# Half of an output projection's first pass placed behind a recurrent scan, and its weights' low parts made on another engine, in a one-core hybrid decoder kernel

## The chip, the cores and the metric

The kernel runs on one core of one Trainium2 chip. The metric is device time in microseconds (us). The engines are named as in the profile: PE (TensorE, matrix products; PEld are its weight loads), DVE (VectorE), ACT (ScalarE), POOL (GpSimd) and SP (SyncE, which here only issues DMAs).

## What is computed

One decoder layer over 512 tokens of width 1024, in float32. A combined input projection feeds three groups of heads side by side; their outputs are concatenated to `y` (512 x 1024) and go through one output projection with a residual, then a squared-ReLU MLP with a residual:

```
h = rms_norm(x, norm_mix[l])
proj = h @ w_in[l]
y_a = gdn_mixer(...)     # 6 heads, gated DeltaNet: a scan over 8 chunks of 64 tokens
y_b = nsa_mixer(...)     # 6 heads of attention: compressed, selected and window branches
y_c = pool_mixer(...)    # 256 columns, causal pooling
y = concatenate([y_a, y_b, y_c], axis=-1)
x = x + y @ w_out[l]
h = rms_norm(x, norm_ffn[l])
x = x + square(relu(h @ w_ffn1[l])) @ w_ffn2[l]
```

Of the columns of `y`, row blocks 0 to 2 of `w_out` (128 rows each) meet the DeltaNet's columns, blocks 3 to 5 the attention's, and blocks 6 and 7 the pooling's.

## The kernel before

A float32 product is made of three products of split operands: each operand is a high part (a cast, on ACT) and a low part (the rest, a subtraction), and the kernel sums high x high, high x low and low x high. So each weight that is loaded goes through a raw buffer, a cast on ACT and a subtraction, before PE can use it.

The program has three stretches. Up to some 233 us PE projects the tokens and solves the DeltaNet's triangular systems (`slabs`, `preps`, `solves`). From there to some 372 us three tracks share the engines: the end of the DeltaNet's scan (`gdn_step`, nine steps, of which steps 4 to 8 fall here), then `gdn_out` for four row tiles of 128 tokens; the attention (`attentions`, `probs`, `values`); and the output projection (`out_gdn`). After that the MLP runs with PE full.

A step of the scan makes six groups of small products on one PSUM bank: `ps` is started (L895, L899), `vn` is copied out by DVE (L903), the next state is made (L912, L915), and the outputs are summed (L920) and copied to `vb` by ACT (L924). `gdn_out` takes a tile of `vb`, normalizes it (L934 to L938, with the tiny steps of `rsqrt` on L103 to L111), multiplies it by the gate on POOL (L939), transposes it on PE into bank 3 (L942), and splits it into `yTh` and `yTl` (L147 on ACT, L148 on DVE), column by column.

The output projection goes in three passes, `PASS = [(6,7),(0,1,2),(3,4,5)]`, each a list of row blocks of `w_out`. A pass has eight tiles (four row tiles by two column halves `hf`); a tile is three products of 128x512 for each block (L1247 in `out_mm`) in one bank, added to `x2` by DVE (L1252). The first pass needs nothing of the scan or the attention; the second needs the DeltaNet's `yTh`, `yTl`.

The weights are loaded by `load_w`: a DMA (L1217) into one of two raw buffers of the pool `wr`, a cast on ACT (L1219), and the low part. For blocks 0 to 5 and for the first two slabs of `w_ffn1` (mode "AG") the low part is two POOL subtractions of 128x512 (L1223); for blocks 6 and 7 (mode "AV") it is one DVE subtraction of 128x1024 (`split`, L134). The parts live in two pools: `wo4` (two blocks) lies beside the DeltaNet's memory `gd`, and `wo6` (three blocks) in memory that `gd` gives back. Before, blocks 4 to 7 are in `wo4`, blocks 0 to 3 in `wo6`.

The order of the instructions on each engine is set by a list scheduler when the program is built: `side_by_side((42, attentions()), (27, out_gdn()))` sets priorities, and the scheduler places each instruction by its own estimate of time. Every engine then runs its list strictly in that order. `tc.issue_after(ins)` orders the instructions that are traced inside it, on the engine of `ins`, behind `ins`; `keep_in_program_order` does the same for a chain.

The lines that the prediction names: L134, L147, L148 (splits), L110 and L111 (`rsqrt`), L895 to L924 (`gdn_step`), L938 to L942 (`gdn_out`), L1097 (compressed probabilities), L1116 to L1122 (scores, their maximum and their exponential), L1145 and L1161 (transposes and value products), L1217 to L1223 (`load_w`), L1247 and L1252 (output products and their additions).

Of the kernel before, what the change touches and what calls it, by code (L numbers as in the profile page):

```python
# [16 lines left out]
ALU = mybir.AluOpType  # L17
# [3 lines left out]
P = 128  # L21
# [16 lines left out]
def trunk_kernel(ctx, tc, x, norm_mix, w_in, conv_w, a_log, dt_bias, gdn_norm, nsa_q_norm, nsa_k_norm,  # L38
# [844 lines left out]
    def gdn_step(t, St):  # L883

        sides = []
        for a in range(2):
            if 0 <= t - a < 2 * NT:
                i, p = divmod(t - a, 2)
                sides.append((grp[i], i, halves[p], halves[1 - p], 3 * a, slice(a, H, 2)))
        rows, nrows = (slice(0, P), slice(0, P)) if len(sides) == 2 else sides[0][2:4]  # L890
        ps = ps_()
        p3 = ps[:, 0:384].rearrange("p (a s c) -> p a s c", a=2, s=3)
        for j in range(3):
            for d, i, h, nh, s0, hs in sides:
                PE.matmul(ps[h, ts(j, HD)], d["TT"][h, s0 + j], vb[h, i, hcol(s0 + j)], start=(j == 0), stop=False,  # L895
                          skip_group_check=True)
        for j in range(3):
            for d, i, h, nh, s0, hs in sides:
                PE.matmul(ps[h, ts(j, HD)], kr[h, i, s0 + j], St[h, j], start=False, stop=(j == 2),  # L899
                          skip_group_check=True)  # L900
        yield 0.4
        vn = w1t([P, 3, HD], "vn")
        V.tensor_copy(vn[rows], p3[rows, 0])  # L903
        Sn = St
        if t < 2 * NT:
            gls = w1t([P, 3, HD], "gls")
            Sn = w1t([P, 3, HD], "S")
            for d, i, h, nh, s0, hs in sides:
                G.tensor_tensor(gls[nh], St[h], egc[h, 2, i, hs].unsqueeze(2).to_broadcast([64, 3, HD]), ALU.mult)
            for j in range(3):  # L910
                for d, i, h, nh, s0, hs in sides:
                    PE.matmul(ps[nh, 192 + HD * j:192 + HD * j + HD], qr[h, i, hcol(s0 + j)], vn[h, j], start=True, stop=True)  # L912
            if t == 0:
                V.memset(Sn[sides[0][2]], 0.0)
            V.tensor_tensor(Sn[nrows], p3[nrows, 1], gls[nrows], ALU.add)  # L915
            yield 0.2
        for a_ in range(2):
            for j in range(3):
                for d, i, h, nh, s0, hs in sides:
                    PE.matmul(ps[h, ts(j, HD)], (d["qdT"][h, s0 // 3, j], d["QK"][h, s0 + j])[a_],  # L920
                              (St[h, j], vn[h, j])[a_], start=(j == 0 and a_ == 0), stop=(j == 2 and a_ == 1),
                              skip_group_check=True)
        for d, i, h, nh, s0, hs in sides:
            S.copy(vb[h, i, hs], p3[h, 0])  # L924
        yield 0.4
        return Sn
# [70 lines left out]
        yield from proj_tok([(0, win[:, 2572:2700]), (128, win[:, 1152:1280])], vw)  # L997
        yield from proj_tok([(0, win[:, 1280:1536])], lambda ps: gate_z(128, ps, ps))

    grp, have = {}, set()  # L1000

    def until(*names):
        while not have.issuperset(names):
# [56 lines left out]
    wr = ctx.enter_context(pool("wr", 2, side="right"))  # L1060
    nwe = ExitStack()
    nw = nwe.enter_context(pool("nw", 2, side="right"))
    wop = [nwe.enter_context(pool("wo4", 4, side="right"))]
    gd.close()
    wop.append(nwe.enter_context(pool("wo6", 6, side="right")))
    fe = ExitStack()
    wq = fe.enter_context(pool("wq", 2))

# [141 lines left out]
    def load_w(pl_, view, tag, e):  # L1210
# [3 lines left out]
        for k in range(0, n, 1024 // m):  # L1214
            k = slice(k, k + 1024 // m)
            r = wr.tile([P, 1024 // m, m], F32, tag="raw", name=nm("raw"))
            SY.dma_start(r, view[:, k])  # L1217
            if e == "AG":
                S.copy(hi[:, k], r)  # L1219
                for d in [(k, slice(d, d + 512)) for d in range(0, m, 512)] if m > 512 else \  # L1220
                        [(slice(q, q + 512 // m), slice(0, m)) for q in range(k.start, k.stop, 512 // m)]:
                    rd = r[:, d[0].start - k.start:d[0].stop - k.start, d[1]]
                    G.tensor_tensor(lo[:, d[0], d[1]], rd, f32v(hi[:, d[0], d[1]]), ALU.subtract)  # L1223
            else:
                split([(r, k)], hi, lo, e)
        return hi, lo

    def load_wo(*cs):
        for c in cs:
            wo[c] = load_w(wop[c < 4], w_out[0, ts(c, P), :].unsqueeze(1), "wo", "AG" if c < 6 else "AV")  # L1230

    w1s = []
    PASS = [(6,7),(0,1,2),(3,4,5)]

    def load_w1(q):
        return load_w(wq, w_ffn1[0, :, 256 * q:256 * q + 256].rearrange("(k p) n -> p k n", p=P), "w1",
                      "AG" if q < 2 else "AV")

    po = banks(4, 5), banks(4, 5, 6), banks(4, 5, 0, 1)

# [23 lines left out]
        begun.append(po[2]())  # L1264
        out_mm(begun[g_], PASS[-1], 0, 2, g_ // 2, g_ % 2, kp)

    def out_part(cl, hf):

        for i in range(NT):
            out_tile(cl, i, hf)  # L1270
            yield 0.64 * len(cl)

    def out_gdn():
        for cl in PASS[:-1]:
            load_wo(*cl)
            if cl is PASS[0]:
                for i in range(NT):
                    SY.dma_start(x2[i], x[0, ts(i, P), :])
            yield from until(*(("y", c) for c in cl if 2 < c < 6))
            for hf in range(2):  # L1280
                yield from out_part(cl, hf)
        load_wo(*PASS[-1])
        have.add("w_out")
        w1s.extend(load_w1(q) for q in range(2))

# [197 lines left out]
```

## Time and profile before

| what | value |
|---|---|
| median of 3 runs | 715.31 us (715.3 to 715.41) |
| the profiled execution | 715.41 us |
| its span, first to last instruction | 713.7 us |
| granted TensorE clock, mean | 0.994 of full speed |
| PE busy | 692.7 us, 97% of the span |
| DVE, ACT, POOL busy | 76%, 55%, 28% of the span |

The profiled execution is 1.7 us longer than its span, and 0.1 us above the median. A row of the timeline gives start, duration, engine, line, operation, output<-inputs, shape and count, and in brackets the idle time before it and what ended it. A row of the windows gives, for a stretch, its length, then busy time and number of instructions of PE, PEld, DVE, ACT and POOL, then the granted clock, the DMA engines' busy share, and GB/s.

### The profile page before, as it was taken

The numbers are of one execution on the slowest core, as the hardware profiler recorded it, in microseconds if no ns is written. First come the engines' busy times: TensorE is split into PE (matmuls) and PEld (weight loads), VectorE is DVE, ScalarE is ACT, GpSimd is POOL, SyncE is SP. The second block draws the span as 40 slices with busy tenths as digits, with TensorE's granted clock in tenths as the row PEclk, the third lists the DMA queues.
The fourth block names the chain that finished last, engine by engine and source line by source line (L and its number), as shares of the span: only waits on it lengthen the run. The fifth ranks groups of instructions, "written<-read, shape, count | busy, mean of one in ns | idle before, by whom it ended". The sixth has DMA issues, their size and how long they took to land.

```text
span 713.7 us, 13238 instructions
## 1 busy us (share of the span) xinstructions
PE 692.7 (97%) x5137; PEld 567.4 (80%) x5137; DVE 544.8 (76%) x999; ACT 392.4 (55%) x786; POOL 200.9 (28%) x277
## 2 busy tenths in 40 slices
PE   8999999999999997999999999999999999999997
PEld 8888777999888775676679888888888888888885
DVE  6688998877786879566566996968878586886836
ACT  5465845665773577388575664446355534635440
POOL 6820023223134013343030242505041230504123
PEclk9999999999999999899999999999999999999999
DMA  7343223133213301211210614233140523322103
GB/s 225 97 133 89 70 51 90 32 108 107 76 32 130 110 1 32 88 59 60 89 54 37 196 71 135 71 119 118 60 141 36 163 73 119 118 60 76 43 1 118
DMA packets 49921, 62.19 MB, mean 87 GB/s; under 512 B 5494, under 2 KB 42564, under 8 KB 49860
## 3 DMA queue, kind: packets, MB, share of 16 engines
q1 hardware_dynamic: 48996, 61.16, 27.4%
q8 instruction: 40, 0.66, 0.4%
q10 hardware_dynamic: 864, 0.20, 0.1%
q14 instruction: 21, 0.17, 0.1%
HBM read 59.25 MB, written 2.10 MB: 86 GB/s over the span
## 4 chain that ended last, share of the span: by engine, by line
PE 85%; DVE 7%; ACT 4%; issue 2%; DMA 2%; POOL 1%; SPq 0%; DVEq 0%; ACTq 0%
PE ps L1344 25%; PE ps L143 10%; PE ps L142 10%; PE ps L144 10%; PE ps L434 6%; PE ps L1247 5%; PE ps L815 3%; PE ps L1161 3%; PE ps L1145 2%; PE ps L260 2%; PE ps L1116 1%; PE ps L603 1%; DMA raw<-in_w_in_dram 1%; PE ps L1117 1%; PE ps L920 1%
## 5 line engine op out<-in xcount | busy, mean ns | idle before, releaser
L1344 PE MATMUL ps<-h2l,hw 128*128 128x512 f32 (+1 forms) x280 | 104.8, 374 | 0.4 <-DVE h2l L1323 0.4
L1344 PE MATMUL ps<-h2h,hw 128*128 128x512 f32 (+1 forms) x280 | 105.2, 376 | 0.0
L1344 PE MATMUL ps<-h2h,lw 128*128 128x512 f32 (+1 forms) x280 | 104.9, 375 | 0.0
L1371 POOL TENSOR_TENSOR al<-gF,ah 128x512 fp32r<-128x512 f32 x24 | 34.3, 1429 | 226.7 <-ACT ah L1370 183.6
L142 PE MATMUL ps<-bh,ah 128*128 128x512 f32 x224 | 88.2, 394 | 0.5 <-DVE x L1452 0.5
L143 PE MATMUL ps<-bl,ah 128*128 128x512 f32 x224 | 88.1, 393 | 0.0
L1452 DVE TENSOR_TENSOR x<-ps,x 128x512 f32<-128x512 f32 x112 | 73.2, 682 | 18.7 <-PE ps L144 18.6
L144 PE MATMUL ps<-bh,al 128*128 128x512 f32 x224 | 84.9, 393 | 0.0
L1364 DVE TENSOR_TENSOR bl<-w2r,bh 128x1024 fp32r<-128x1024 f32 x40 | 57.4, 1436 | 5.6 <-ACT bh L1363 5.6
L1344 PEld LDWEIGHTS ps<-h2l,hw 128*128 128x128 f32 x280 | 52.7, 188 | 10.8 <-DVE h2l L1323 0.6
L1371 POOL TENSOR_TENSOR al<-gS,ah 128x512 fp32r<-128x512 f32 x32 | 56.6, 1788 | 15.8 <-ACT ah L1370 15.8
L1344 PEld LDWEIGHTS ps<-h2h,lw 128*128 128x128 f32 x280 | 52.6, 188 | 10.5
L1344 PEld LDWEIGHTS ps<-h2h,hw 128*128 128x128 f32 x280 | 52.5, 188 | 10.2
L1363 ACT CAST bh<-w2r 128x1024 fp32r<-128x1024 f32 x40 | 41.7, 1048 | 33.4 <-PE ps L144 33.2
L133 ACT CAST hi<-raw 128x512 fp32r<-128x512 f32 (+1 forms) x76 | 36.9, 522 | 25.2 <-PE ps L143 8.5
L142 PEld LDWEIGHTS ps<-bh,ah 128*128 128x128 f32 x224 | 42.1, 188 | 10.5 <-ACT ah L1370 0.8
L134 DVE TENSOR_TENSOR lo<-raw,hi 128x512 fp32r<-128x512 f32 (+1 forms) x76 | 43.8, 596 | 8.0 <-ACT hi L133 7.1
L144 PEld LDWEIGHTS ps<-bh,al 128*128 128x128 f32 x224 | 42.1, 188 | 9.7
L143 PEld LDWEIGHTS ps<-bl,ah 128*128 128x128 f32 x224 | 42.1, 188 | 9.7
L1370 ACT CAST ah<-gS 128x512 fp32r<-128x512 f32 x32 | 19.9, 622 | 39.6 <-DVE gS L1434 19.9
L143 PE MATMUL ps<-hTl,hi 128*128 128x512 f32 x104 | 41.3, 398 | 0.0
L133 ACT CAST hw<-raw 128x1024 fp32r<-128x1024 f32 x28 | 28.1, 1046 | 23.8 <-PE ps L1344 23.8
(378 smaller groups left out, 1698.2 us busy)
## 6 DMA issues: line engine op xcount, KB each, us to landing
raw<-in_w_ffn_dram SPq DMA_DIRECT2D x32, 512.0 KB, 3.9
w2r<-in_w_ffn_dram SPq DMA_DIRECT2D x32, 512.0 KB, 4.5
raw<-in_w_in_dram SPq DMA_DIRECT2D x24, 256.0 KB, 2.9
raw<-in_w_in_dram SPq DMA_DIRECT2D x36, 128.0 KB, 2.6
x<-in_x_dram SPq DMA_DIRECT2D x8, 512.0 KB, 6.1
raw<-in_cmp_w_dram SPq DMA_DIRECT2D x32, 128.0 KB, 2.4
raw<-in_w_out_dram SPq DMA_DIRECT2D x8, 512.0 KB, 3.8
out_dram<-x SPq DMA_DIRECT2D x8, 256.0 KB, 2.0
```

Of the source, the lines that this page charges most:

```text
L133: {"A": S.copy, "V": V.tensor_copy, "G": G.tensor_copy}[e[0]](hi[:, k], r)
L134: {"V": V, "G": G}[e[1]].tensor_tensor(lo[:, k], r, f32v(hi[:, k]), ALU.subtract)
L142: PE.matmul(ps, ah, bh, start=start, stop=False, **kw)
L143: PE.matmul(ps, ah, bl, start=False, stop=False, **kw)
L144: PE.matmul(ps, al, bh, start=False, stop=stop, **kw)
L434: PE.matmul(ps[:, ts(i, 256)], a_[:, k, ts(2 * b + i, P)], w_, start=(k == 0 and n_ == 0 and i == 0), stop=(k == KC - 1 and n_ == 2 and i ...
L1247: keep(PE.matmul(ps, a_[c][:, ts(i, P)], wo[c][w_][:, 0, cs], start=n_ == 0 and m_ == 0, stop=n_ == len(cl) - 1 and m_ == 2))
L1344: keep(PE.matmul(ps[:, tok], w[w_][:, k, ts(f, P)], a_[k][:, tok], start=k == 0 and m_ == 0, stop=k == KC - 1 and m_ == 2))
L1363: S.copy(hi, src)
L1364: V.tensor_tensor(lo, src, f32v(hi), ALU.subtract)
L1371: G.tensor_tensor(lo, src, f32v(hi), ALU.subtract)
L1452: V.tensor_tensor(x2[i][:, cs], acc[bk, t_], x2[i][:, cs], ALU.add)
```

## The change

The change does three things. The four tiles of the first pass's second half (`hf` = 1) are traced under `tc.issue_after(scan_end[-1].ins)`, so that their products stand on PE behind the scan's last product (L921 in the new numbering; lines behind it are shifted by +1, and by -7 from `load_w` on). Every low part of `w_out` and of the first slabs of `w_ffn1` is made by one DVE subtraction, and the POOL form is gone. The two pools change places: `wo6`, beside the DeltaNet's memory, holds blocks 6, 7 and 0, and later 3, 4 and 5; `wo4`, in the memory given back, holds blocks 1 and 2. `out_gdn` is written out as a list of steps, and the second pass's blocks are loaded before the first pass's second half.

```diff
@@ gdn_step
-                    PE.matmul(ps[h, ts(j, HD)], (d["qdT"][h, s0 // 3, j], d["QK"][h, s0 + j])[a_],
+                    scan_end.append(
+                        PE.matmul(ps[h, ts(j, HD)], (d["qdT"][h, s0 // 3, j], d["QK"][h, s0 + j])[a_],
...
-    wop = [nwe.enter_context(pool("wo4", 4, side="right"))]
+    wop = [nwe.enter_context(pool("wo6", 6, side="right"))]
     gd.close()
-    wop.append(nwe.enter_context(pool("wo6", 6, side="right")))
+    wop.append(nwe.enter_context(pool("wo4", 4, side="right")))
...
             SY.dma_start(r, view[:, k])
-            if e == "AG":
-                S.copy(hi[:, k], r)
-                for d in [(k, slice(d, d + 512)) for d in range(0, m, 512)] if m > 512 else \
-                        [(slice(q, q + 512 // m), slice(0, m)) for q in range(k.start, k.stop, 512 // m)]:
-                    rd = r[:, d[0].start - k.start:d[0].stop - k.start, d[1]]
-                    G.tensor_tensor(lo[:, d[0], d[1]], rd, f32v(hi[:, d[0], d[1]]), ALU.subtract)
-            else:
-                split([(r, k)], hi, lo, e)
+            split([(r, k)], hi, lo, e)
...
-            wo[c] = load_w(wop[c < 4], w_out[0, ts(c, P), :].unsqueeze(1), "wo", "AG" if c < 6 else "AV")
+            wo[c] = load_w(wop[c in (1, 2)], w_out[0, ts(c, P), :].unsqueeze(1), "wo", "AV")
...
     def out_gdn():
-        for cl in PASS[:-1]:
-            load_wo(*cl)
-            if cl is PASS[0]:
-                for i in range(NT):
-                    SY.dma_start(x2[i], x[0, ts(i, P), :])
-            yield from until(*(("y", c) for c in cl if 2 < c < 6))
-            for hf in range(2):
-                yield from out_part(cl, hf)
-        load_wo(*PASS[-1])
+        load_wo(*PASS[0])
+        for i in range(NT):
+            SY.dma_start(x2[i], x[0, ts(i, P), :])
+        for i in range(NT):
+            out_tile(PASS[0], i, 0)
+            yield 0.64 * 2
+        load_wo(*PASS[1])
+        for i in range(NT):
+            with tc.issue_after(scan_end[-1].ins):
+                out_tile(PASS[0], i, 1)
+            yield 0.64 * 2
+        for i in range(2 * NT):
+            out_tile(PASS[1], i % NT, i // NT)
+            yield 0.64 * 3
+        load_wo(3, 4, 5)
```

The scheduler moves more than the diff tells. Three places follow, with the rows of the built programs.

The first is PE at the scan's last product (output `ps_3407`). Before, it stands among the attention's scores (`ps_5008`) and transposes (of `P`), and the DeltaNet's first output transpose (L942) follows:

```order
L920 MATMUL ps_3407<-vn_3414,QK_1491 64x64 x3
L1145 MATMUL ps_4917<-ident,P_4794 128x128
L1145 MATMUL ps_4917<-ident,P_4819 128x128
L1116 MATMUL ps_5008<-XT_4041,XT_3562 128x512
L1117 MATMUL ps_5008<-XT_4042,XT_3562 128x512
L1118 LDWEIGHTS identb
L1118 MATMUL ps_5008<-negb,identb 128x128
L1145 MATMUL ps_4940<-ident,P_4845 128x128
L1145 MATMUL ps_4940<-ident,P_4870 128x128
L1145 MATMUL ps_4940<-ident,P_4880 128x128
L1145 MATMUL ps_4940<-ident,P_4897 128x128
L942 MATMUL ps_4344<-ident,vb 128x128 x3
```

Now two tiles of the first pass follow it at once (the second, `ps_4823`, begins here); the other two, `ps_4874` and `ps_4921`, come 15 rows later, behind the first L943:

```order
L921 MATMUL ps_3407<-vn_3414,QK_1491 64x64 x3
L1240 MATMUL ps_4765<-hwo_4528,yTh_3075 128x512
L1240 MATMUL ps_4765<-lwo_4529,yTh_3075 128x512
L1240 MATMUL ps_4765<-hwo_4528,yTl_3076 128x512
L1240 MATMUL ps_4765<-hwo_4534,yTh_3488 128x512
L1240 MATMUL ps_4765<-lwo_4535,yTh_3488 128x512
L1240 MATMUL ps_4765<-hwo_4534,yTl_3489 128x512
L1240 MATMUL ps_4823<-hwo_4528,yTh_3075 128x512
```

So 24 products of 128x512 moved from the scan's steps to behind the scan. Two groups of scores that stood ahead of the last product stand behind it now as well.

The second place is ACT as the attention begins. Before, the first exponentials (L1122) follow the last DeltaNet evictions (`kr`) and the compressed probabilities (`pc`):

```order
L133 CAST hwo_4534<-raw_4536 128x1024
L880 ACTIVATE kr<-ps_3008 128x384
L1091 ACTIVATE pc_4498<-pc_4498 128x384
L880 ACTIVATE kr<-ps_3025 128x384
L1122 ACTIVATE P_4526,sm_4519<-ps_4520,mx_4524 128x128
L1122 ACTIVATE P_4558,sm_4519<-ps_4552,mx_4556 128x256
```

Now block 0's cast (`hwo_4747`) stands ahead of them:

```order
L880 ACTIVATE kr<-ps_3008 128x384
L1092 ACTIVATE pc_4498<-pc_4498 128x384
L880 ACTIVATE kr<-ps_3025 128x384
L133 CAST hwo_4747<-raw_4749 128x1024
L1123 ACTIVATE P_4526,sm_4519<-ps_4520,mx_4524 128x128
L1123 ACTIVATE P_4558,sm_4519<-ps_4552,mx_4556 128x256
```

On DVE its low part stands in the same way just ahead of the scaling of `pc` and the scan's copy `vn`:

```order
L1097 TENSOR_TENSOR sm_4497<-sm_4497,vld 128x3
L134 TENSOR_TENSOR lwo_4748<-raw_4749,hwo_4747 128x1024
L1098 TENSOR_TENSOR pc_4498<-pc_4498,sm_4497 128x384
L903 COPY vn_3260<-ps_3247 128x192
L1245 TENSOR_TENSOR x_4448<-ps_4544,x_4448 128x512
L1245 TENSOR_TENSOR x_4449<-ps_4612,x_4449 128x512
```

So the cast and the low part of block 0, which stood behind the scan, moved to its middle.

The third place is DVE behind the scan, where the DeltaNet's last rows are normalized (`ss`, `rs`, `r`) and the first row tile's `yTl` are made. Before, only tiny steps and small evictions stand here:

```order
L111 SCALAR_TENSOR_TENSOR r_4414<-rs_4419,r_4414 128x6
L148 TENSOR_TENSOR yTl_3242<-ps_4344,yTh_3241 128x128
L109 TENSOR_TENSOR rs_4419<-r_4414 128x6
L1081 TENSOR_TENSOR s_5032<-ps_5033,ngcb_178 128x192
L110 TENSOR_TENSOR rs_4419<-rs_4419,ss_4413 128x6
L1082 TENSOR_TENSOR s_5032<-ps_5033,s_5032 128x192
```

Now low parts of 128x1024 and additions to `x2` stand between them:

```order
L134 TENSOR_TENSOR lwo_4754<-raw_4755,hwo_4753 128x1024
L1121 TENSOR_REDUCE mx_4992<-ps_4988 128x1
L109 TENSOR_TENSOR rs_4419<-r_4414 128x6
L134 TENSOR_TENSOR lwo_4760<-raw_4761,hwo_4759 128x1024
L148 TENSOR_TENSOR yTl_3242<-ps_4344,yTh_3241 128x128
L1245 TENSOR_TENSOR x_4450<-ps_4874,x_4450 128x512
L110 TENSOR_TENSOR rs_4419<-rs_4419,ss_4413 128x6
L1245 TENSOR_TENSOR x_4451<-ps_4921,x_4451 128x512
L148 TENSOR_TENSOR yTl_3244<-ps_4344,yTh_3243 128x128
```

From the scan's last `vn` to the last `yTl` of the fourth row tile, DVE's list gained five low parts (blocks 1, 2, 3 and 4 and half a slab of `w_ffn1`) and four additions; four more low parts come behind. On ACT the cast of block 3 stands between the second and the third `yTh` of the first row tile, and all four casts of the two slabs of `w_ffn1` come before the fifth head's scores, where before two of them came behind.

## Rows read from the trace of the kernel before

**Rows 1.** The page's first part, busy time and share by engine.
```profile
PE 692.7 (97%) x5137; PEld 567.4 (80%) x5137; DVE 544.8 (76%) x999; ACT 392.4 (55%) x786; POOL 200.9 (28%) x277
```

**Rows 2.** Windows: five stretches from the scan's end to the attention's end.
```profile
244.00:256.40 12.40, 12.40 (x96) 9.51 (x95) 9.52 (x30) 6.53 (x19) 2.03 (x3) 1.00 0.01 1
256.40:275.60 19.20, 18.84 (x245) 14.74 (x243) 15.06 (x49) 16.08 (x45) 1.01 (x2) 1.00 0.01 2
...
275.60:302.00 26.40, 20.69 (x93) 14.60 (x93) 19.50 (x53) 11.99 (x32) 12.04 (x10) 0.87 0.24 77
302.00:320.00 18.00, 17.99 (x97) 13.51 (x97) 12.18 (x27) 14.07 (x30) 6.08 (x5) 1.00 0.21 63
320.00:350.00 30.00, 27.00 (x150) 18.85 (x149) 19.23 (x45) 24.69 (x62) 9.58 (x8) 1.00 0.28 88
```

**Rows 3.** Timeline of PE behind the scan's end.
```profile
280.80 0.50 PE L1247 MATMUL ps<-lwo,yTh 128*128 128x512 f32 x1 [0.72 <-POOL lwo L1223]
...
283.63 0.45 PE L1116 MATMUL ps<-XT,XT 128*128 128x128 f32 x1 [2.11 <-DVE s L1082]
```

**Rows 4.** Windows: ten microseconds behind the scan's end.
```profile
280.00:285.00 5.00, 1.60 (x6) 1.01 (x5) 5.00 (x10) 1.76 (x4) 4.43 (x4) 0.72 0.31 106
285.00:290.00 5.00, 4.73 (x16) 3.08 (x16) 3.87 (x14) 2.85 (x8) 1.75 (x2) 0.59 0.33 106
```

**Rows 5.** Timeline of DVE in the same stretch, tiny steps of 128x6.
```profile
279.53 1.24 DVE L111 SCALAR_TENSOR_TENSOR r<-rs,r 128x6 f32<-128x6 f32 x1
...
282.19 1.03 DVE L110 TENSOR_TENSOR rs<-rs,ss 128x6 f32<-128x6 f32 x1
...
285.02 0.15 DVE L110 TENSOR_TENSOR rs<-rs,ss 128x6 f32<-128x6 f32 x1
```

**Rows 6.** Timeline of POOL in the same stretch.
```profile
279.44 4.99 POOL L1223 TENSOR_TENSOR lwo<-raw,hwo 128x512 fp32r<-128x512 f32 x4 [1.25 <-ACT hwo L1219]
```

**Rows 7.** Timeline of PE: output products within the scan, and the scan's last products.
```profile
245.47 0.39 PE L1247 MATMUL ps<-lwo,yTh 128*128 128x512 f32 x1
...
247.33 0.39 PE L1247 MATMUL ps<-hwo,yTh 128*128 128x512 f32 x1
...
275.13 0.51 PE L920 MATMUL ps<-vn,QK 64*64 64x64 f32 x6
```

**Rows 8.** SP's issue of block 0's transfer, and the tile view of `raw`.
```profile
233.34 2.65 SPq L1217 DMA_DIRECT2D raw<-in_w_out_dram  x2
...
DMA to landing us min/median/max: 3.6/3.8/4.5
```

**Rows 9.** Timelines of ACT, DVE and PE as the attention begins.
```profile
236.34 0.37 ACT L1122 ACTIVATE P<-ps,mx 128x128 f32<-128x128 f32 x1 [0.89 <-DVE mx L1120]
...
237.02 0.56 DVE L1097 TENSOR_TENSOR pc<-pc,sm 128x384 f32<-128x384 f32 x1
237.50 0.35 DVE L903 COPY vn<-ps 128x192 f32<-128x192 f32 x1
...
238.78 0.56 PE L912 MATMUL ps<-vn,qr 64*64 64x64 f32 x12
...
239.46 0.48 PE L1247 MATMUL ps<-hwo,yTh 128*128 128x512 f32 x1
```

**Rows 10.** DVE: one low part; groups by form, 228 to 375 us; a window.
```profile
232.10 1.21 DVE L134 TENSOR_TENSOR lwo<-raw,hwo 128x1024 fp32r<-128x1024 f32 x1
...
L1252 DVE TENSOR_TENSOR x<-ps,x 128x512 f32<-128x512 f32 x24 | 16.2, 686 | 4.9 <-PE ps L1247 4.8
...
274.20:299.80 25.60, 19.89 (x98) 13.86 (x99) 20.82 (x56) 13.39 (x35) 12.04 (x10) 0.87 0.19 62
```

**Rows 11.** Timeline of ACT: casts of weights in the attention's second half.
```profile
303.10 1.05 ACT L1219 CAST hwo<-raw 128x1024 fp32r<-128x1024 f32 x1 [3.66 <-DMA raw<-in_w_out_dram]
...
325.29 1.05 ACT L1219 CAST hw<-raw 128x1024 fp32r<-128x1024 f32 x1
...
333.87 1.04 ACT L1219 CAST hw<-raw 128x1024 fp32r<-128x1024 f32 x1
```

More of the change, by code (lines that the diff above doesn't have):

```diff
@@ L919, in gdn_step @@
                 for d, i, h, nh, s0, hs in sides:
-                    PE.matmul(ps[h, ts(j, HD)], (d["qdT"][h, s0 // 3, j], d["QK"][h, s0 + j])[a_],
-                              (St[h, j], vn[h, j])[a_], start=(j == 0 and a_ == 0), stop=(j == 2 and a_ == 1),
-                              skip_group_check=True)
+                    scan_end.append(
+                        PE.matmul(ps[h, ts(j, HD)], (d["qdT"][h, s0 // 3, j], d["QK"][h, s0 + j])[a_],
+                                  (St[h, j], vn[h, j])[a_], start=(j == 0 and a_ == 0), stop=(j == 2 and a_ == 1),
+                                  skip_group_check=True))
         for d, i, h, nh, s0, hs in sides:
@@ L998, in slabs @@
         yield from proj_tok([(0, win[:, 1280:1536])], lambda ps: gate_z(128, ps, ps))
-    grp, have = {}, set()
+    grp, have, scan_end = {}, set(), []
     def until(*names):
@@ L1235, in load_w1 @@
     def load_w1(q):
-        return load_w(wq, w_ffn1[0, :, 256 * q:256 * q + 256].rearrange("(k p) n -> p k n", p=P), "w1",
-                      "AG" if q < 2 else "AV")
+        return load_w(wq, w_ffn1[0, :, 256 * q:256 * q + 256].rearrange("(k p) n -> p k n", p=P), "w1", "AV")
     po = banks(4, 5), banks(4, 5, 6), banks(4, 5, 0, 1)
@@ L1265, in out_begin, with out_gdn @@
         out_mm(begun[g_], PASS[-1], 0, 2, g_ // 2, g_ % 2, kp)
-    def out_part(cl, hf):
+    def out_gdn():
+        load_wo(*PASS[0])
         for i in range(NT):
-            out_tile(cl, i, hf)
-            yield 0.64 * len(cl)
-    def out_gdn():
-        for cl in PASS[:-1]:
-            load_wo(*cl)
-            if cl is PASS[0]:
-                for i in range(NT):
-                    SY.dma_start(x2[i], x[0, ts(i, P), :])
-            yield from until(*(("y", c) for c in cl if 2 < c < 6))
-            for hf in range(2):
-                yield from out_part(cl, hf)
-        load_wo(*PASS[-1])
+            SY.dma_start(x2[i], x[0, ts(i, P), :])
[11 more added lines that the diff above has]
+        load_wo(3, 4, 5)
         have.add("w_out")
```

## The prediction

> **What bounds the kernel now.** I read the page's first part first: PE is busy 97% of the span [rows 1], so the end is set by PE's list, and a change can gain only what PE idles or runs slowly. Then the windows by stage: the only stretch with real idle time is the one behind the scan. From 275.6 to 302 PE is busy 20.69 of 26.40 us [rows 2], 5.7 us idle. Before it PE is full (12.40 of 12.40, then 18.84 of 19.20), behind it too until 320; from 320 to 350 it loses 3.0 of 30 us, with ACT busy 24.69 [rows 2].
>
> Next, what PE waits for there: first the low part of a `w_out` block from POOL (0.72 us), then a scaled score `s` from DVE (2.11 us) [rows 3]. DVE is the engine behind most of it: from 280 to 285 it is busy 5.00 of 5.00 us while PE does 1.60 [rows 4]. Part of that is not work: a step on 128x6 that takes 0.15 us takes 1.24 and 1.03 just then [rows 5], beside a row of four POOL subtractions that last 4.99 us together [rows 6]. Five steps are stretched so, by about 0.9 each, some 4.5 us of DVE time.
>
> The idle time costs PE a second time. The granted clock falls to 0.72 in the five microseconds in which PE does 1.60, and is 0.59 in the next five, in which it is busy 4.73 [rows 4]: near the 1.2 GHz level, half of full speed. Over the 26.40 us it is 0.87 [rows 2], so about 0.13 of 20.69 us of busy time, some 2.7 us, is lost to it; I count 2.3, since the idle part weighs in the mean. The prize is thus at most 5.7 + 2.3 = 8 us.
>
> **The change part by part.** *The 24 products moved behind the scan.* Before, they stand between the scan's steps; eight of them start between 245.47 and 247.33 (the ninth's start) [rows 7], so one is 1.86 / 8 = 0.23 us and the 24 are 5.6 us. PE is full there, so each later scan step can come earlier, and the scan's last products, which begin at 275.13 and end at 275.64 [rows 7], come up to 5.6 us earlier. The 5.6 us are paid again behind the scan, in the gap: by itself this is neutral for PE's sum, and gains exactly as much of the gap as gets filled. Whether it does is decided by DVE, whose last `vn`, at 274.20, I take as the start of its stretch [rows 10].
>
> *Block 0 early.* Its low part now stands on DVE ahead of `pc` and `vn`, which ran at 237.02 and 237.50 [rows 9]. Its transfer can be issued as blocks 6's and 7's successor at 233.34; the landing takes 3.8 us by the median (3.6 to 4.5) [rows 8], so 237.1; the cast is 1.05 [rows 11], the low part 1.21 [rows 10]: 239.4. So `pc` starts 2.4 us late and `vn` ends at 239.4 + 0.56 + 0.35 = 240.3, not 237.85; the scan's products on it (L912, 238.78) and the output product that follows (239.46) [rows 9] wait to about 240.4 and 241.0. The exponential of 236.34 on ACT [rows 9] stands behind the cast, so it is 1.9 us late too. PE has 1.3 to 2.6 us that nothing covers, since its list is in order; I take 1.9. With it the scan ends 5.6 - 1.9 = 3.7 earlier, near 272.
>
> *DVE behind the scan.* From 274.20 to 299.80 (the last `yTl` of the fourth tile) DVE is busy 20.82 of 25.60 us [rows 10]. Out go the 4.5 us of stretching, since POOL's subtractions are gone. In come five low parts of 1.21 (6.1), four additions of 0.686 (2.7) [rows 10], and about 1.1 of score steps that were ahead of the last product: 20.82 - 4.5 + 6.1 + 2.7 + 1.1 = 26.2 us of work. Waits were 4.8; part of them were for steps that now have other work in front, so I take 2.2 (from 0 to 4.8). So the stretch is 28.4 us (26.2 to 31.0) instead of 25.6, and starts 3.7 us earlier: it ends 0.9 us earlier (3.1 earlier to 1.7 later). That is all that is left of 8 us: DVE is what holds the rest.
>
> *The clock* is in that number and not beside it: if PE runs on its 24 products while it waited before, the fall to 0.59 goes, but PE then waits for the same DVE.
>
> *Behind it.* Two casts of `w_ffn1` (325.29 and 333.87, 1.05 each [rows 11]) leave the stretch in which ACT is busy 24.69 of 30 us and PE loses 3.0 [rows 2]; they come earlier, where ACT is half idle (11.99 of 26.40). Against this four more low parts (4.8 us) are on DVE, which is busy 19.23 of 30 there [rows 2]. I take 0.7 us as gain, a third of the 2.1 us that the casts occupy, since not every exponential stands behind one; at best 2.1, at worst 2.5 lost, half of the low parts' time. The moved loads on SP's queue cost nothing: the DMA engines are busy 0.24 at most in these stretches [rows 2]. That cover goes if a raw buffer is late, which is a rival below.
>
> **Sum.** 0.9 to 1.0 behind the scan and 0.7 later, 1.7 us from 715.41, the profiled execution, which is 0.1 above the median: 713.7 us.
>
> A rule of the Trainium skill bears on the stretched steps. "SBUF — State Buffer", section "SBUF: two separate sides", says that DVE and GpSimd share one port pair, that an instruction of DVE with two SBUF inputs takes it from a GpSimd instruction that reads SBUF, or the other way round, and holds it to its end as a lock. Rows 5 and 6 agree (1.24 and 1.03 against 0.15), for DVE as the one that waits. By the same rule a DVE low part would now hold a POOL product of the gate for up to 1.21 us, which no row here shows; four such holds would take back at most 4.8 us.
>
> **Rivals.** *R1, the gap is filled.* DVE's waits vanish and its list, of 26.2 us, is ordered so that PE never needs what is last on it. For it: 3.7 us of the 5.7 idle us lie in the 280 to 285 window and its neighbour, in which the stretching sits, and the clock stays up. Against it: DVE has no spare time by the sum above. It gives 3.1 + about 1.5 behind: 4.6 us, 710.8.
>
> *R2, ACT blocked by a raw buffer: slower.* There are two raw buffers, and one is held long by block 5, so that the loads behind run on one: low part done, transfer 3.8, cast 1.05, low part 1.21, together 6.1 us a block. ACT runs in order, and now the cast of block 3 stands ahead of the third `yTh` of the first row tile, and the slabs' casts ahead of the last scores. Before, one such cast already waits 3.66 us for its DMA [rows 11], with little behind it. The rival decides when that wait begins before ACT has done what PE needs, which is from the second low part's delay on: a wait of 3.66 in place of the 1.7 gained is 2.0 us slower, 717.4. For it: DVE, which now frees the raw buffers, is busy 5.00 of 5.00 [rows 4]. Against it: the loads start earlier, too.
>
> *R3, DVE gives all back: no change.* DVE's waits stay at 4.8, so that its stretch ends 1.7 later, and 1.7 us are won by casts and clock: 715.3. For it: DVE is the engine that is full in the gap [rows 4], and it is given 9 us. The Trainium skill has the rule behind this ("Perfetto Trace Analysis", section "Optimizing Scalar/DVE Operations"): when DVE is saturated, work may be moved to Scalar or even GPSIMD, with the warning that GPSIMD shares a port with DVE. This change goes the other way. By that rule the time would not fall; by its warning, the 4.5 us of stretching come off, and the trace has both.
>
> **How the numbers follow.** A measurement of this kernel can tell about 0.2% from no change, 1.4 us. The forecast has 0.42, R1 0.21, R2 0.18, R3 0.19. The forecast's own spread (3.1 earlier to 1.7 later behind the scan) puts some 0.26 of its 0.42 beyond 1.4 us faster and the rest within. Faster is 0.26 + 0.21 = 0.47, slower 0.18 and 0.02 of R3, 0.20, the same 0.33. The likeliest case gives 713.7. The range goes from 710.3, half a microsecond below R1, to 717.2, just short of R2's 717.4: the likeliest own range (712 to 715.5) is inside, and the two tails left out, half of R2 and a part of R1, are under 0.2.
>
> **What would show it.** Right: the scan's last product ends near 272; block 0's cast on ACT begins at about 237.1 after a wait for a DMA, with PE short of work by 1.3 to 2.6 us near 240; the 128x6 steps of L110 and L111 back near 0.15; DVE almost full from 271 to 299; the granted clock near 1.00 from 276 to 302; POOL's busy time less by the subtractions. R1 shows if PE is full from 276 to 302 and the MLP starts over 4 us earlier; R2 if a cast on ACT waits over 3 us for `raw` with an exponential or a `yTh` behind it and PE idle meanwhile; R3 if PE's idle time from 276 to 302 stays near 5 us. The forecast is wrong if block 0's wait on the DMA is absent, if DVE's stretch from the last `vn` takes under 26 or over 31 us, or if another stretch of the program than those in rows 2 changes its length by over 1 us.

## The result and the profile after

Before 715.52 us (median of 12 runs), after 711.85 us (12 runs): ratio 0.9946, 95% interval 0.9931 to 0.996, so 3.7 us faster. Of the change's 12 runs, the eight with a mean granted clock of 0.999 or 1.000 take 711.41 to 711.90 us, and the four with 0.995 to 0.998 take 712.76 to 714.79. The profiled execution of the change takes 711.84 us with a span of 709.9 us, against 715.41 and 713.7.

The page's first part [rows 1], then windows: one of the kernel before and one of the changed kernel, each from the start of the scan's last products to the first product with `pcT` behind them, and two of five microseconds of the changed kernel:

```profile
PE 689.6 (97%) x5137; PEld 565.8 (80%) x5137; DVE 550.8 (78%) x1009; ACT 392.2 (55%) x786; POOL 175.1 (25%) x257
```

```profile
275.13:302.04 26.91, 21.20 (x101) 14.98 (x100) 19.97 (x54) 12.46 (x33) 12.04 (x10) 0.87 0.24 76
...
271.65:299.16 27.51, 24.65 (x132) 18.70 (x130) 23.64 (x68) 14.69 (x37) 1.00 (x1) 1.00 0.27 81
...
280.00:285.00 5.00, 5.00 (x33) 4.05 (x31) 4.45 (x13) 3.12 (x6) 0.00 (x0) 1.00 0.53 141
285.00:290.00 5.00, 3.76 (x17) 2.15 (x15) 5.00 (x21) 2.98 (x9) 0.00 (x0) 1.00 0.60 197
```

POOL lost the 25.8 us of its low parts. Behind the scan PE idles 2.86 of 27.51 us where it idled 5.71 of 26.91, and the granted clock stays at 1.00 through the whole stretch, full speed; before it was 0.87, with 0.72 and 0.59 between 280 and 290 [rows 4].

The timeline of the changed kernel near 240 us (ACT, DVE, PE) answers to rows 9:

```profile
237.46 1.05 ACT L133 CAST hwo<-raw 128x1024 fp32r<-128x1024 f32 x1 [1.87 <-DMA raw<-in_w_out_dram]
238.41 0.36 ACT L1123 ACTIVATE P<-ps,mx 128x128 f32<-128x128 f32 x1
...
238.54 1.23 DVE L134 TENSOR_TENSOR lwo<-raw,hwo 128x1024 fp32r<-128x1024 f32 x1 [1.41 <-ACT hwo L133]
239.68 0.55 DVE L1098 TENSOR_TENSOR pc<-pc,sm 128x384 f32<-128x384 f32 x1
240.15 0.35 DVE L903 COPY vn<-ps 128x192 f32<-128x192 f32 x1
...
238.92 0.44 PE L1117 MATMUL ps<-XT,XT 128*128 128x384 f32 x1 [1.14 <-ACT P L1123]
240.86 0.56 PE L912 MATMUL ps<-vn,qr 64*64 64x64 f32 x12
241.36 0.50 PE L1240 MATMUL ps<-hwo,yTh 128*128 128x512 f32 x1
...
271.65 0.51 PE L921 MATMUL ps<-vn,QK 64*64 64x64 f32 x6
```

Block 0's cast waits 1.87 us for its transfer, and the exponential behind it is 2.1 us late, `pc` 2.7, PE's products on `vn` 2.1 (240.86, not 238.78), and the output product behind them 1.9 (241.36, not 239.46). Of each, 0.14 us were there at 231 us already (table below). The scan's last products begin at 271.65, 3.48 us earlier than at 275.13 [rows 7].

Behind the scan, DVE, PE and POOL of the changed kernel (POOL by groups, 228 to 375 us):

```profile
276.18 1.22 DVE L134 TENSOR_TENSOR lwo<-raw,hwo 128x1024 fp32r<-128x1024 f32 x1
277.31 0.55 DVE L1121 TENSOR_REDUCE mx<-ps 128x1 f32<-128x384 f32 x1
...
280.66 0.15 DVE L111 SCALAR_TENSOR_TENSOR r<-rs,r 128x6 f32<-128x6 f32 x1
...
296.18 1.22 DVE L134 TENSOR_TENSOR lw<-raw,hw 128x1024 fp32r<-128x1024 f32 x1 [0.71 <-ACT hw L133]
...
286.20 0.36 PE L1117 MATMUL ps<-XT,XT 128*128 128x256 f32 x1 [0.85 <-DVE s L1083]
292.16 0.51 PE L1240 MATMUL ps<-hwo,yTh 128*128 128x512 f32 x1 [1.26 <-DVE x L1245]
```

```profile
L940 POOL TENSOR_TENSOR vb<-vb,zt 128x384 f32<-128x384 f32 x3 | 3.0, 999 | 31.8 <-DVE vb L939 31.8
```

The 128x6 steps take 0.15 us again [rows 5]. PE's longest waits are 0.85 and 1.26 us, not 2.11 [rows 3]. POOL's gate product takes 999 ns. The three start at 254.60, 270.18 and 291.19, and no low part on DVE runs beside one of them, so these rows do not test whether a low part would hold them.

For all kernels below I use three marks of PE's timeline: the scan's last products, the first product with `pcT` behind them (here called the end of the gap), and the first transpose of `xn` ahead of the MLP. "Tail" is from the second to the third. "From 231" is the time to the first mark from the scan's products on `vb` and `LT` (L895) near 231 us. Up to there the kernels execute the same instructions, yet the profiled executions arrive there up to 1.3 us apart (ac's 3.6 us late), which the instructions do not explain; so what an edit did within the scan is read from this column. Each mark comes from one execution. Times in us.

| kernel | median | ratio (95%) | scan's last | from 231 | gap | tail |
|---|---|---|---|---|---|---|
| before | 715.52 | 1 | 275.13 | 43.76 | 26.91 | 63.27 |
| the change | 711.85 | 0.9946 (0.9931 to 0.996) | 271.65 | 40.14 | 27.51 | 62.08 |
| a_issue | 711.3 | 0.9942 (0.9921 to 0.9963) | 269.55 | 38.49 | 27.03 | 63.98 |
| ab | 715.74 | 1.0002 (0.9989 to 1.0014) | 269.82 | 38.49 | 31.36 | 63.15 |
| ac | 716.3 | 1.0013 (0.9994 to 1.0032) | 274.80 | 39.82 | 33.08 | 62.85 |
| bc | 717.35 | 1.0024 (1.0009 to 1.0038) | 276.42 | 44.98 | 28.97 | 62.19 |
| ab_dup12 | 716.95 | 1.0023 (1.0014 to 1.0031) | 270.06 | 38.50 | 30.96 | 65.53 |
| d_late0 | 711.32 | 0.9945 (0.9933 to 0.9957) | 270.20 | 39.35 | 28.13 | 62.15 |
| a36 | 717.18 | 1.0021 (1.0012 to 1.003) | 268.83 | 37.59 | 32.18 | 65.62 |
| f_w1pool | 712.65 | 0.9962 (0.995 to 0.9974) | 271.29 | 40.14 | 27.23 | 62.97 |
| after_wr3 | 719.95 | 1.0064 (1.0052 to 1.0076) | 273.70 | 42.65 | 27.08 | 67.96 |
| ab_wr3 | 721.45 | 1.0084 (1.0063 to 1.0105) | 271.28 | 39.17 | 32.00 | 66.40 |
| d_late0_wr3 | 717.09 | 1.0019 (1.0008 to 1.003) | 272.99 | 41.55 | 27.56 | 66.58 |
| a_issue_wr3 | 720.36 | 1.0064 (1.0052 to 1.0077) | 271.63 | 40.75 | 33.52 | 64.99 |

So the change won 3.48 us up to the scan's end (3.62 from 231), paid 0.60 in the gap, which took in 24 products and two groups of scores more, and won 1.19 in the tail. The MLP behind is 0.27 longer, and together that is the 3.8 us by which the span is shorter.

### The profile page after: what moved, and what is told of

It reads as the page before. It is cut to its first block, busy times and chain, and to the rows that moved or that the text cites. A ratio compares the mean times of both kernels' runs of the same rounds, so it can differ in the third digit from the quotient of the medians.

```text
span 709.9 us, 13231 instructions
## 1 busy us (share of the span) xinstructions
PE 689.6 (97%) x5137; PEld 565.8 (80%) x5137; DVE 550.8 (78%) x1009; ACT 392.2 (55%) x786; POOL 175.1 (25%) x257
## 2 busy tenths in 40 slices
DMA packets 49921, 62.19 MB, mean 88 GB/s; under 512 B 5494, under 2 KB 42564, under 8 KB 49860
## 4 chain that ended last, share of the span: by engine, by line
PE 85%; DVE 6%; ACT 4%; DMA 2%; issue 2%; POOL 1%; SPq 0%; DVEq 0%; POOLq 0%; ACTq 0%
PE ps L1337 25%; PE ps L144 10%; PE ps L143 10%; PE ps L142 10%; PE ps L434 6%; PE ps L1240 4%; PE ps L815 3%; PE ps L1162 2%; PE ps L1146 2%; PE ps L260 2%; PE ps L603 1%; DMA raw<-in_w_out_dram 1%; PE ps L1117 1%; DMA raw<-in_w_in_dram 1%; PE ps L921 1%
## 5 line engine op out<-in xcount | busy, mean ns | idle before, releaser
L133 ACT CAST hw<-raw 128x1024 fp32r<-128x1024 f32 x32 | 32.2, 1046 | 24.5 <-PE ps L1337 23.9
L134 DVE TENSOR_TENSOR lw<-raw,hw 128x1024 fp32r<-128x1024 f32 x32 | 39.1, 1255 | 8.0 <-ACT hw L133 7.8
```

The costliest lines, as they stand in the source:

```text
L133: {"A": S.copy, "V": V.tensor_copy, "G": G.tensor_copy}[e[0]](hi[:, k], r)
L134: {"V": V, "G": G}[e[1]].tensor_tensor(lo[:, k], r, f32v(hi[:, k]), ALU.subtract)
```

## The experiments

The change has three parts: the first orders 24 products behind the scan, the second moves the low parts to DVE, the third gives block 0 another home (and loads the second pass's blocks earlier in the list). Four runs combine them. Line numbers of these kernels differ by a few from those above.

### One part, and each pair

*a_issue*, the first part alone, on the kernel before:

```diff
             for hf in range(2):
-                yield from out_part(cl, hf)
+                if cl is PASS[0] and hf:
+                    for i in range(NT):
+                        with tc.issue_after(scan_end[-1].ins):
+                            out_tile(cl, i, hf)
+                        yield 0.64 * len(cl)
+                else:
+                    yield from out_part(cl, hf)
```

> The kernel before with one part of the change alone: the four tiles of the first pass's second half are ordered on PE behind the scan's last product; the low parts stay on POOL, the pools stay where they were. Theory 1 (the gap pays): the 24 products, 5.6 us, leave a full stretch and fill idle time, the granted clock stays at full speed, and since block 0's cast is not brought forward there is no hold near 240 us. The scan ends 5.6 us earlier, the MLP starts 3 to 5 us earlier: 710.5 to 712.5. Rival (the parts need each other): without early low parts the second pass waits for POOL (cast, two subtractions of 1.28 us, one block every 7.4 us), PE idles as long as before behind the moved products, and the gain stays under 1.4 us: 714.1 to 715.5.

711.3 us: the first part alone gives what the whole change gives. The scan ends 5.58 us earlier, 5.27 of it from 231 on, near the 5.6 of 24 products, and the gap is 27.03 us with these products in it, 26.91 without. The rival is out. The gap's clock is 1.00 throughout, although DVE's small steps are still stretched (1.22 us beside POOL's subtractions). The tail is 0.7 us longer than before, and the rows (ACT, then PE, then windows) show why:

```profile
319.10 1.04 ACT L1220 CAST hw<-raw 128x1024 fp32r<-128x1024 f32 x1 [1.40 <-DMA raw<-in_w_ffn_dram]
320.05 0.58 ACT L147 CAST pt<-ps 128x512 fp32r<-128x512 f32 x1
...
320.68 0.58 PE L1162 MATMUL ps<-pt,Vt 128*128 128x512 f32 x1 [1.74 <-ACT pt L147]
```

```profile
315.00:320.00 5.00, 3.94 (x25) 2.79 (x24) 2.78 (x6) 3.43 (x9) 0.44 (x1) 1.00 0.34 105
320.00:325.00 5.00, 4.22 (x19) 3.46 (x19) 3.13 (x7) 3.60 (x11) 2.51 (x2) 0.66 0.21 59
```

A cast waits for a transfer, a `pt` that PE needs stands behind it on ACT, PE waits 1.74 us, and the clock falls to 0.66.

*ab*, the first part with the low parts on DVE (`"AV"` for every weight in `load_w`'s calls):

> The change without its third part: products ordered behind the scan and low parts on DVE, but block 0 in the memory that the DeltaNet gives back, so that its load waits for the scan's end. Theory 1 (block 0's early cast costs 2.1 us near 240 and buys less): the scan ends 5.6 instead of 3.5 us earlier, and the second pass waits for block 0 under 1 us, since transfer, cast and low part are 6.1 us and the moved products 5.6 us: 709.8 to 711.3, faster than the whole change. Rival (the early block is needed): the low parts of blocks 0 to 2 come one behind the other after the scan, about 3.8 us apart for the raw buffers, and PE waits for the third: 712.5 to 714.

715.74 us, slower than theory and rival said. The scan ends as early as with the first part alone, and the gap is 4.3 us longer. ACT and PE, then windows:

```profile
285.26 1.04 ACT L133 CAST hwo<-raw 128x1024 fp32r<-128x1024 f32 x1 [2.01 <-DMA raw<-in_w_out_dram]
286.21 0.36 ACT L1123 ACTIVATE P<-ps,mx 128x128 f32<-128x128 f32 x1
...
286.72 0.44 PE L1117 MATMUL ps<-XT,XT 128*128 128x384 f32 x1 [1.61 <-ACT P L1123]
...
292.05 0.63 PE L1247 MATMUL ps<-hwo,yTh 128*128 128x512 f32 x1
```

```profile
285.00:290.00 5.00, 3.21 (x13) 1.88 (x12) 4.19 (x12) 2.70 (x8) 0.63 (x1) 0.80 0.23 66
290.00:296.00 6.00, 4.32 (x10) 2.97 (x11) 4.01 (x10) 1.48 (x3) 0.37 (x1) 0.60 0.30 101
```

This is the prediction's R2 at work: in a_issue the fourth cast behind the scan (289.28) stands behind these exponentials, here it stands ahead of them, and it waits 2.01 us for its transfer. That the scheduler puts it earlier because the low part on DVE is done sooner than POOL's two is likely, but not tested. PE waits 1.61 us, its clock falls, and a run of products takes 0.43 us each (0.63 is the length of one, they overlap) instead of 0.23.

*ac*, the first and third part, low parts on POOL (the change with the `"AG"` branch kept):

> The change without its second part: products ordered behind the scan, block 0 outside the DeltaNet's memory and loaded early, low parts on POOL as before. Theory 1 (what counts on DVE is its sum): 4.5 us of stretched steps come back and 6.1 us of low parts go, so DVE is about even, and the low part of block 0 no longer holds the scan, of which 1.0 of the 2.1 us near 240 come back: 711 to 712.5. Rival (POOL's rate and the shared stretching decide): a block takes 7.4 us for cast and POOL, and each of DVE's small steps beside it takes about 1 us instead of 0.15: 713 to 715.

716.3 us: the rival, and more. The profiled execution (721.13 us) is 4.8 us over the median. It lost some 3.6 us ahead of 231, at a granted clock of 0.97 between 100 and 200 us, and up to 1.2 us behind, so its gap may be that much too long; only differences inside it are used. DVE, POOL and PE:

```profile
289.76 2.43 DVE L1090 TENSOR_TENSOR pc<-s,mx 128x128 f32<-128x128 f32 x2
...
288.20 5.12 POOL L1224 TENSOR_TENSOR lwo<-raw,hwo 128x512 fp32r<-128x512 f32 x4
...
293.58 0.80 PE L1248 MATMUL ps<-hwo,yTl 128*128 128x512 f32 x1 [2.65 <-DVE yTl L148]
```

```profile
295.00:300.00 5.00, 4.22 (x13) 2.77 (x12) 2.96 (x7) 0.68 (x3) 0.00 (x0) 0.50 0.26 88
```

With block 0 out of the way the blocks behind it come in pairs, 1 with 2 and 3 with 4, and the second pair's four subtractions on POOL fall on a place where DVE has a step with two SBUF inputs and PE's next `yTl` behind it. The two `pc` steps take 2.43 us (three take 0.7 in the change), PE waits 2.65, and runs at half speed afterwards.

*bc*, the second and third part, the products where the scheduler puts them:

> The change without its first part: low parts on DVE and block 0 early, but the products of the first pass's second half where the scheduler puts them. Theory 1 (the moved products are the gain): PE is full before the scan's end and idles behind it, now with more work on DVE there; block 0 still holds the scan by about 2 us: 716 to 718.5, slower than the kernel before. Rival (the gain is that POOL leaves): the stretching is gone, and PE's gap shrinks by 2 to 4 us without any moved product: 712 to 714.

717.35 us, as theory 1 said: the scan ends 1.3 us later than before, since block 0 holds it, and the gap, without POOL's subtractions, is 2.1 us longer, with the clock down to 0.50 from 295 to 300. Taking the stretching away did not shorten the gap here. So the first part is needed for the gain, and by a_issue it is enough; with only one of the other two beside it the gain is lost.

### Does more work in the gap cost anything?

*ab_dup12*:

```diff
+                    for i in range(2):
+                        with tc.issue_after(scan_end[-1].ins):
+                            out_mm(po[0](), cl, 0, 2, i, 1)
+                        yield 0.64 * len(cl)
```

> Products behind the scan and low parts on DVE, block 0 late (the kernel of the second run), plus 12 products of 128x512 more, 2.8 us of PE's work: two tiles of the first pass are computed a second time behind the scan into a bank that nobody reads. Theory 1 (the clock): in that kernel PE waited 1.61 us for an exponential behind a cast, was busy 3.21 of 5 us, and then ran its products at 0.43 us each instead of 0.23, at a granted clock of 0.6 from 290 to 296; work that keeps PE busy into that place keeps the clock at 1.00. The added 2.8 us lie in its 4.5 us of waits and the 2.4 us of clock come back: 712.5 to 714, faster with more work. Rival (PE's waits are set by DVE and ACT behind the scan, and the clock is a symptom): no change or up to 2.8 us slower: 715.4 to 718.5.

716.95 us, inside the rival's range. In the gap theory 1 half holds: with 2.8 us more of products it is 0.4 us shorter (30.96 against 31.36), and the clock is 1.00 where it was 0.80. But PE then waits for a `yTl`, and the fall comes there:

```profile
294.95 0.52 PE L943 MATMUL ps<-ident,vb 128*128 128x128 f32 x3 [2.73 <-DVE yTl L148]
```

```profile
290.00:295.00 5.00, 2.27 (x10) 1.57 (x11) 4.29 (x11) 1.48 (x3) 0.00 (x0) 1.00 0.25 96
295.00:300.00 5.00, 4.65 (x15) 3.60 (x16) 1.50 (x4) 1.84 (x4) 0.00 (x0) 0.66 0.35 108
```

The tail is 2.4 us longer, in an order that the scheduler changed too. The gap took the added work and grew no longer; that the clock alone makes the difference between the two kernels is not shown.

*a36*, the first part with 36 products (`hf == 0`, `i >= 2` ordered behind the scan as well):

> The kernel before with the first part alone, and more of it: 36 instead of 24 products behind the scan (the second half's four tiles and two of the first half's). Theory 1 (the stretch behind the scan is as long as DVE's work in it, and PE still idles 3.4 us there): the scan ends 2.8 us earlier than with 24, DVE gets two additions more, 1.2 us: 709.3 to 710.6. Rival A (PE's idle time behind is set by block 0's way through cast and POOL, and is filled): the 2.8 us are paid back, 711 to 712. Rival B (block 0's transfer starts when the scan ends, and its casts meet other work on ACT): a long wait and a fall of the clock, 713 to 716.

717.18 us, 5.9 us slower than with 24, a miss. The scan ends only 0.7 us earlier (0.9 from 231), where the 12 products were priced at 2.8: PE now waits there for ACT and DVE (0.56, 0.31, 0.24 and 0.74 us). And the gap is 32.18 us at a clock of 1.00 in every window. DVE and PE:

```profile
272.71 1.20 DVE L110 TENSOR_TENSOR rs<-rs,ss 128x6 f32<-128x6 f32 x1
...
275.18 1.20 DVE L109 TENSOR_TENSOR rs<-r 128x6 f32<-128x6 f32 x1
...
276.70 0.69 DVE L1253 TENSOR_TENSOR x<-ps,x 128x512 f32<-128x512 f32 x1
...
277.44 0.50 PE L1248 MATMUL ps<-hwo,yTh 128*128 128x512 f32 x1 [1.48 <-DVE x L1253]
297.19 0.50 PE L1248 MATMUL ps<-hwo,yTh 128*128 128x512 f32 x1 [1.71 <-ACT yTh L147]
```

The addition that frees a bank stands behind stretched steps, and later a `yTh` behind a cast that waits 2.05 us for its transfer. The gap can be made long by waits alone, without a fall of the clock.

### Parts of the change: block 0's cast, the slabs, the raw buffers

*d_late0*: in `load_w`, for block 0 alone,

```diff
-            split([(r, k)], hi, lo, e)
+            with ExitStack() as late:
+                if late0:
+                    late.enter_context(tc.issue_after(scan_vb[8].ins))
+                    late.enter_context(tc.issue_after(scan_vn[5].ins))
+                split([(r, k)], hi, lo, e)
```

So on ACT its cast stands behind the copy to `vb` of the scan's step 4, and on DVE its low part behind the copy `vn` of step 5.

> The whole change, with one order more: block 0's cast stands on ACT behind the copy of the scan's step 4, and its low part on DVE behind the scan's copy of step 5, so that neither waits near 240 us for the transfer. Theory 1 (the early cast holds the scan for 2.1 us): PE's wait of 1.14 us at 238.92 is gone, the scan's last product comes 1.5 to 2.1 us earlier, near 269.8, and the rest keeps its length: 709.5 to 710.5. Rival A (other work covers it): within 0.7 us of the whole change, 711.2 to 712.5. Rival B (everything behind is shifted against the raw buffers, PE waits over 1.6 us in one place and the granted clock falls again): 713 to 716.

711.32 us, in rival A's range. The wait at 238.92 is gone and the scan ends 1.45 us earlier, but 0.66 of that was there at 231, ahead of the edit; 0.79 is the edit's, about half of what theory 1 said. 0.62 us is given back in the gap, where the clock falls behind waits of PE of 0.59 (at 283.53) and 0.80 us:

```profile
285.37 0.50 PE L1244 MATMUL ps<-hwo,yTl 128*128 128x512 f32 x1 [0.80 <-DVE yTl L148]
```

```profile
280.00:285.00 5.00, 3.92 (x20) 2.84 (x19) 4.76 (x14) 3.13 (x5) 0.00 (x0) 1.00 0.56 192
285.00:290.00 5.00, 4.63 (x16) 3.18 (x16) 4.80 (x19) 1.86 (x7) 1.01 (x1) 0.66 0.36 109
```

*f_w1pool*: the change with `"AG" if q < 2 else "AV"` kept in `load_w1`.

> The whole change, but the low parts of the first two slabs of w_ffn1 on POOL as before, those of w_out on DVE. Theory 1 (the 1.2 us won between 299 and 329 us come from the casts, which come earlier, and not from DVE): a slab's raw buffer is freed 1.4 us later by POOL, nothing else changes up to 299 us: 711.5 to 712.5. Rival A (DVE's four low parts there cost PE time): 710.0 to 711.2. Rival B (with POOL's rate the casts are late again, and the 1.2 us are lost): 712.7 to 713.5.

712.65 us; up to the gap's end it stands 0.64 us better than the change, and its tail is 0.89 us longer. Of the 0.64, 0.36 was there at 231, and the scan takes the same 40.14 from there. The lists of the two kernels are the same up to the gap's end but for the change's low part at 296.18, and 0.17 of the other 0.28 us come behind that one. By these two executions some 0.9 of the 1.19 us won in the tail go with the slabs' low parts on DVE, and the casts' place alone does not give them: rival A is out, and the truth lies between theory 1 and rival B.

*ab_wr3, after_wr3, d_late0_wr3, a_issue_wr3*: each with

```diff
-    wr = ctx.enter_context(pool("wr", 2, side="right"))
+    wr = ctx.enter_context(pool("wr", 3, side="right"))
```

> Products behind the scan and low parts on DVE, block 0 late (the kernel of the second run), with three raw buffers for weights instead of two. Theory 1 (ACT's cast waits 2.01 us for a transfer at 285.26 with an exponential and a yTh queued behind it; PE then waits 1.61 us for that exponential, and the granted clock falls to 0.6): with a buffer more the transfers start earlier, the wait and the fall go, and the stretch behind the scan is 27 to 28.5 us instead of 31.4: 711 to 713. Rival (the late block itself, or DVE, holds PE): 714.5 to 716, and the stretch stays over 30 us.

> The whole change with three raw buffers instead of two. Theory 1 (with block 0 in its own home only one cast waits over 1 us on ACT, 1.50 at 281.07, and nothing that PE needs is late by it): no gain behind the scan; the slabs' casts come earlier: 711 to 712.2, within 0.7 us of the whole change. Rival (the transfers still set the second pass and DVE's order): 708.5 to 710.5.

> The whole change with block 0's cast and low part ordered later in the scan, and three raw buffers. Theory 1 (the later cast won 1.45 us at the scan's end, of which 0.6 us went to a fall of the clock to 0.66 at 285 to 290 behind a PE wait of 0.80 us for a yTl; with the transfers earlier this fall goes): 709.5 to 711. Rival (the fall stays, or another comes): 711 to 714.

> The first part alone, with three raw buffers. Theory 1 (POOL's two subtractions set the rate of the blocks there; the one long wait is PE's 1.74 us at 320.68 for a pt copy that stands on ACT behind a cast that waits for its transfer, and it takes the clock to 0.94 from 320 to 350): that wait goes: 709.5 to 710.7. Rival (POOL's rate): no change, 711 to 712; or, with casts that come in other places on ACT, slower: 713 to 716.

All four are 5.7 to 9.1 us slower than with two buffers, more than any theory had it. In after_wr3 the gap is as short as ever (27.08), the scan ends 2.1 us later (2.5 from 231) and the tail is 5.9 us longer. ACT and PE of after_wr3, then a window:

```profile
236.81 1.04 ACT L133 CAST hwo<-raw 128x1024 fp32r<-128x1024 f32 x1 [2.42 <-DMA raw<-in_w_out_dram]
...
238.19 0.47 ACT L880 ACTIVATE kr<-ps 128x384 f32<-128x384 f32 x1
...
238.71 0.50 PE L1240 MATMUL ps<-hwo,yTh 128*128 128x512 f32 x1 [2.11 <-ACT kr L880]
...
301.75 1.05 ACT L133 CAST hw<-raw 128x1024 fp32r<-128x1024 f32 x1 [2.21 <-DMA raw<-in_w_ffn_dram]
302.70 0.58 ACT L147 CAST pt<-ps 128x512 fp32r<-128x512 f32 x1
305.39 1.05 ACT L133 CAST hw<-raw 128x1024 fp32r<-128x1024 f32 x1 [2.11 <-DMA raw<-in_w_ffn_dram]
...
306.98 0.44 PE L1162 MATMUL ps<-pt,Vt 128*128 128x384 f32 x1 [0.90 <-ACT pt L147]
```

```profile
310.00:315.00 5.00, 5.00 (x22) 3.63 (x23) 3.22 (x10) 2.98 (x7) 0.00 (x0) 0.78 0.13 46
```

The buffer does not shorten the waits: the scheduler puts the casts earlier, ahead of more of what PE needs (block 0's ahead of `kr`, the slabs' ahead of `pt`), and they wait 2.1 to 2.4 us there. That a spare buffer would end the wait in ab was my theory, and it falls; ab's gap is 32.00 with it. In d_late0_wr3, where block 0's cast alone is held back, the fall of the clock in d_late0's gap is gone, as its theory had it, but from 231 the scan is 2.2 us longer and the tail 4.4. What would happen with all casts held back and three buffers was not tried.

## Why the prediction was right, and where it was off

The sign was right and the time, 711.85, lies in the range, 1.9 us below the forecast and 1.1 us above R1. But the gain of 3.7 us is over twice the 1.7 of the sum: the range held it because it reached down past R1, not because the sum was close. By the prediction's own signs, R1's is half there: the MLP starts 4.07 us earlier (361.24, not 365.31), but PE is not full from 276 to 302 (23.14 of 26.00 us). Point by point:

- *The 24 products and block 0.* Here the sum was right term by term. From 231 to the scan's end the time fell by 3.62 us; the forecast was 3.7. The 24 products alone gave 5.27 (a_issue and ab; forecast 5.6), and block 0's early load took back 1.65 (the change against ab, which lacks the third part; forecast 1.9, from 1.3 to 2.6). d_late0, which holds back its cast and low part alone, got 0.79 of that again.
- *DVE behind the scan.* Here the forecast failed in size. It said 28.4 us (26.2 of work, 2.2 of waits), ending 0.9 us earlier; the row says 27.40 with 24.39 of work and 3.0 of waits, ending 1.6 us earlier:

```profile
270.80:298.20 27.40, 24.53 (x133) 18.65 (x134) 24.39 (x69) 15.40 (x40) 1.37 (x2) 1.00 0.25 77
```

  The durations in the sum overlap: the low part of 276.18 is listed with 1.22 us, and the next step starts 1.13 later; nine added instructions make some 0.8 us of that, and where the other 1.0 us of work went is open. And the gap's end is not DVE's last step: PE reaches it 0.96 us behind that step, before 2.24 (299.80 to 302.04). The fifth low part, at 296.18, stands where PE has products to run, and cost it some 0.17 us of its 1.2 (f_w1pool is without it). The gap took in the 24 products for 0.60 us, where the forecast had charged 2.8 (3.7 less 0.9). "DVE is what holds the rest" was the wrong step.
- *"The clock is in that number and not beside it."* The trace does not bear this out. From mark to mark PE is busy 24.65 us where it was busy 21.20, 3.45 more, though the 24 products alone are 5.6 and two groups of scores came in as well. So over 2 us of busy time came back with the clock (1.00, not 0.87); this is an estimate from these rows. The forecast had 2.3 us for the clock in its count of the prize and none in its sum. In the kernel before, DVE itself waited for scores that PE ran at half speed:

```profile
289.45 0.69 DVE L1120 TENSOR_REDUCE mx<-ps 128x1 f32<-128x512 f32 x1 [1.10 <-PE ps L1118]
```

- *Behind the gap.* Forecast 0.7 us, measured 1.19, of which some 0.9 by the low parts on DVE and the order that comes with them (f_w1pool), which the forecast had counted as a loss, and about 0.3 left for the casts. The DMA engines' "0.24 at most" was a misreading: the rows have 0.28 from 320 to 350 [rows 2].
- *The rivals.* R1's mechanism, a gap that fills while the clock stays up, is nearer to what happened than the forecast's. R2 did not decide here (the cast of 281.07 waits 1.50 us, and no wait of PE over 0.3 us follows before 286), but it is real: ab, a_issue and after_wr3 show it. R3 is out.

By the Trainium skill ("SBUF — State Buffer", "SBUF: two separate sides") DVE and GpSimd hold their shared ports against each other: the stretched steps are 0.15 us again without POOL's low parts, and 1.20 in a36 and 2.43 (for two) in ac with them. The hold of POOL by DVE that the rule also allows agrees with one pair of rows (POOL, DVE): the gate product of 223.67, which starts just behind a DVE step with two SBUF inputs, takes 1.40 us where the three later ones take 1.00. The kernel before has the same pair, with 1.41.

```profile
223.67 1.40 POOL L940 TENSOR_TENSOR vb<-vb,zt 128x384 f32<-128x384 f32 x1
...
223.63 0.56 DVE L858 TENSOR_TENSOR IX<-id,X 128x384 f32<-128x384 f32 x1
```

A low part beside a gate product did not occur in the change, so the prediction's 4.8 us were not put to the test.

What remains open: which wait brings the clock down. In d_late0 it fell behind waits of 0.59 and 0.80 us, in the change it did not behind 0.85 and 1.26, and in a36 it did not behind 1.71. So that the 24 products kept the clock up is what a_issue and the change show side by side with the kernel before; by what amount of work it is kept up, no run here tells.

No version beat the change for certain: a_issue (711.3) and d_late0 (711.32) are 0.5 us faster by their medians, with intervals that overlap its own. For the same time a_issue needs the first part only.

## What to carry to other kernels

A gap behind a dependent chain can take work that does not depend on the chain: ordering 24 ready products behind the scan's last one brought the scan's end over 5 us forward at almost no cost in the gap, and half as many again lost it all. Ask of every load that comes earlier what stands behind its cast on an engine that runs in order: a cast that waits 2 us for a transfer holds an exponential, and PE with it. And price a wait of PE twice where the granted clock can fall behind it.

## What the runs showed that I had not expected

Parts of a change do not add up: the first alone gives 0.58%, each pair nothing or a loss of up to 0.24%, all three 0.54%. A third buffer for weights cost 0.8 to 1.3% of the time, and the casts' waits did not get shorter by it, while their order changed. And in ab_dup12 the gap was 0.4 us shorter with 12 products more in it.
